# First SwiGLU of a hybrid encoder block: seven block products in place of eight, and the down product in passes over tokens

## The chip, the core and the metric

One core of a Trainium2 chip runs the whole block in one launch. The metric is the device time of one execution in microseconds. TensorE does the matrix products (PE in the profile, its weight loads PEld), VectorE (DVE), ScalarE (ACT) and GpSimd (POOL) the elementwise work, and SyncE (SP) issues most transfers between DRAM and the on-chip memory.

## The reference

One layer on 1024 tokens of width 1024: a SwiGLU half-step, a mixer (differential attention beside a bidirectional state-space part), a second SwiGLU half-step, a norm. The change is in the first SwiGLU:

```python
def swiglu(x, w_gate, w_up, w_down):
    return (jax.nn.silu(x @ w_gate) * (x @ w_up)) @ w_down
...
f = swiglu(rmsnorm(h, p["ffn1_pre_g"]), p["ffn1_w_gate"], p["ffn1_w_up"], p["ffn1_w_down"])
h = h + 0.5 * rmsnorm(f, p["ffn1_post_g"])
m = hybrid_mixer(rmsnorm(h, p["mix_pre_g"]), layer_idx, p)
```

The inner width is 2816, so gate and up are 1024 x 2816 and down is 2816 x 1024, all in float32.

## The kernel before

Every float32 product is made of three matmuls: an operand is split into a rounded part (hi, a CAST on ACT, line 127) and the rest (lo, a subtraction on DVE, line 128), and `mm3` (lines 130 to 135) adds hi·hi, hi·lo and lo·hi in PSUM. One matmul takes 128 rows of the sum and gives 128 x 512 outputs; there are 8 such rows of the width 1024 and 22 column tiles of 128 in the width 2816.

The first SwiGLU (`ffn`) goes over 11 chunks of two column tiles. In a chunk the gate and up weights, 128 x 1024 each, are loaded (`unit`, line 118), split, and multiplied with the transposed normed tokens, which lie on the chip as two halves of 512 tokens (`hT`). Products `pg` and `pu` (lines 230 to 235) have 24 matmuls each. The gate goes through silu on ACT (line 237), is multiplied by up on DVE (line 238) and split into `g`; then `down` (lines 242 to 256) multiplies `g` by two row tiles of the down weight, 12 matmuls for each tile of 128 tokens, and DVE adds the result to an accumulator on the chip (line 256). The first and the last chunk go in quarters of 256 tokens, so that the norms ahead (`norm_T`: Square on ACT, two small POOL steps, a scaling on DVE at line 161, eight transposes on PE at line 168) and the residual behind (`residual`, lines 187 to 193) lie among products. The column block z of the next projection (`proj_z`, 352 columns per matmul) fills in at the end, and `proj_conv` (product `pp`) follows.

A scheduler sets the order of the instructions on each engine. Each engine runs its own in that order and waits in place.

Of the kernel before, what the change touches and what calls it, by code (L numbers as in the profile page):

```python
# [91 lines left out]

class Kernel:
# [62 lines left out]
    def norm_T(self, pool, ps, h, xn, t, gain, halves, tag="pt"):  # L156
# [7 lines left out]
        for q in range(2):  # L164
            pt = ps.tile([P, 4, P], F32, tag=tag, name=tag, bufs=2)
# [897 lines left out]
def build(tc, a, out, stages="all"):  # L1063
    nc = tc.nc
    with ExitStack() as top:
# [15 lines left out]
        def norm_pools(ctx):  # L1081
            return k.pool(ctx, "nrm"), k.pool(ctx, "gains")
# [7 lines left out]
        ring = Ring(rp, 2, rp, 5, more=zp)  # L1090
        with ExitStack() as c1:
            nrm, gains = norm_pools(c1)
            ps = k.pool(c1, "ps1", space=PSUM)
# [195 lines left out]
```

## Time and profile before

| | |
|---|---|
| median of 3 runs | 2681.29 us (2681.08 to 2683.89) |
| the profiled execution | 2680.65 us, its span 2678.9 us |
| PE busy | 2584.6 us, 96% of the span |
| DVE, ACT, POOL busy | 1398.6, 905.1, 660.5 us |
| first SwiGLU and z, first product to first `pp` | 14.14 to 800.68 us |

The first and the last us of the span are its first and last instruction. A matmul's row has its start and a duration that runs on under the next one, so the pace of PE is read from the distance of two starts. Line numbers are those of the kernel above.

### The profile page before, as it was taken

How to read it: one execution, taken by the hardware profiler on the slowest of the kernel's cores; microseconds unless marked ns; L12 is line 12 of the kernel's file. 1: busy time of each engine (PE TensorE's matmuls, PEld its weight loads, DVE VectorE, ACT ScalarE, POOL GpSimd, SP SyncE). 2: the span in 40 equal slices, each digit the busy share in tenths (PEclk: the TensorE clock that was granted, in tenths of full speed). 3: DMA queues.
4: the chain of work that ended last, by engine and by line, in shares of the span. 5: the costliest groups of instructions: out<-in, count | busy, mean ns of one | idle time of the engine just before them, and what ended most of it. 6: DMA issues, size and time to landing. Idle time of an engine off the chain costs nothing.

```text
span 2678.9 us, 33127 instructions
## 1 busy us (share of the span) xinstructions
PE 2584.6 (96%) x13104; PEld 2186.3 (82%) x13104; DVE 1398.6 (52%) x1995; ACT 905.1 (34%) x1523; POOL 660.5 (25%) x644
## 2 busy tenths in 40 slices
PE   8999999999999999999988999999999999999996
PEld 7888888888988889777767888888888888888885
DVE  4233333333474743677637888888732333333336
ACT  4311111111144543444426555555431111111113
POOL 2000000000140184343426666666400000000005
PEclk9999999999999999999999999999999999999998
DMA  5211111111142465655454444442321111111112
GB/s 181 63 47 48 48 48 51 51 48 47 41 153 96 129 214 206 207 188 182 150 162 118 124 112 115 118 123 79 138 94 38 48 48 47 48 47 48 50 46 102
DMA packets 110652, 261.37 MB, mean 98 GB/s; under 512 B 11169, under 2 KB 51745, under 8 KB 105633
## 3 DMA queue, kind: packets, MB, share of 16 engines
q1 hardware_dynamic: 92160, 197.65, 22.6%
q0 software_dynamic: 10016, 57.42, 7.9%
q10 hardware_dynamic: 8320, 4.19, 0.5%
q8 instruction: 103, 1.69, 0.3%
q14 instruction: 53, 0.43, 0.1%
HBM read 191.32 MB, written 67.90 MB: 97 GB/s over the span
## 4 chain that ended last, share of the span: by engine, by line
PE 82%; DVE 6%; ACT 3%; POOL 3%; DMA 3%; issue 3%; SPq 0%; DVEq 0%; POOLq 0%; ACTq 0%
PE po L133 6%; PE po L135 6%; PE po L134 6%; PE pg L133 6%; PE pg L134 6%; PE pg L135 6%; PE pu L134 6%; PE pu L135 6%; PE pu L133 6%; PE pp L133 5%; PE pp L135 5%; PE pp L134 5%; PE pgu L133 2%; PE pgu L135 2%; PE pgu L134 2%
## 5 line engine op out<-in xcount | busy, mean ns | idle before, releaser
L256 DVE TENSOR_TENSOR acc<-acc,po 128x512 f32<-128x512 f32 x320 | 217.3, 686 | 433.4 <-PE po L135 433.0
L152 POOL TENSOR_SCALAR rstd<-rstd 128x1 f32<-128x1 f32 x64 | 30.4, 475 | 1451.4 <-ACT junk L151 1450.8
L128 DVE TENSOR_TENSOR split<-raw,split 128x1024 fp32r<-128x1024 f32 (+1 forms) x133 | 161.5, 1220 | 172.8 <-ACT split L127 172.8
L133 PE MATMUL pu<-hT,split 128*128 128x512 f32 (+1 forms) x624 | 223.6, 358 | 1.5 <-DVE sg L238 1.5
L133 PE MATMUL pg<-hT,split 128*128 128x512 f32 (+1 forms) x624 | 224.6, 360 | 0.3 <-ACT hT L127 0.2
L134 PE MATMUL pg<-hT,split 128*128 128x512 f32 (+1 forms) x624 | 224.4, 360 | 0.0
L135 PE MATMUL pg<-hT,split 128*128 128x512 f32 (+1 forms) x624 | 223.9, 359 | 0.0
L134 PE MATMUL pu<-hT,split 128*128 128x512 f32 (+1 forms) x624 | 223.4, 358 | 0.0
L135 PE MATMUL pu<-hT,split 128*128 128x512 f32 (+1 forms) x624 | 223.1, 358 | 0.0
L127 ACT CAST g<-sg 128x512 fp32r<-128x512 f32 (+1 forms) x104 | 57.5, 553 | 481.6 <-DVE sg L238 189.5
L127 ACT CAST split<-raw 128x1024 fp32r<-128x1024 f32 (+1 forms) x136 | 138.7, 1025 | 237.7 <-PE pu L135 83.6
L800 ACT ACTIVATE e<-sc,st 128x1024 f32<-128x1024 f32 x128 | 143.5, 1121 | 164.5 <-DVE st L796 159.9
L133 PE MATMUL pp<-hT,split 128*128 128x512 f32 x384 | 153.6, 400 | 9.5 <-DVE o L665 9.5
L238 DVE TENSOR_TENSOR sg<-sg,pu 128x512 f32<-128x512 f32 (+1 forms) x104 | 62.9, 605 | 185.4 <-PE pu L135 184.7
L796 DVE TENSOR_REDUCE st<-sc 128x1 f32<-128x1024 f32 x128 | 150.7, 1218 | 12.6 <-PE sc L794 12.5
L135 PE MATMUL pp<-hT,split 128*128 128x512 f32 x384 | 152.2, 396 | 0.0
L134 PE MATMUL pp<-hT,split 128*128 128x512 f32 x384 | 151.8, 395 | 0.0
L237 ACT ACTIVATE sg<-pg 128x512 f32<-128x512 f32 (+1 forms) x104 | 55.3, 532 | 271.2 <-PE pg L135 271.1
L133 PE MATMUL po<-odd,g 128*128 128x512 f32 x352 | 138.8, 396 | 6.8 <-DVE acc L256 6.8
L134 PE MATMUL po<-split,g 128*128 128x512 f32 x352 | 139.0, 395 | 0.0
L133 PE MATMUL po<-split,g 128*128 128x512 f32 x352 | 138.9, 396 | 0.1
L135 PE MATMUL po<-odd,g 128*128 128x512 f32 x352 | 138.4, 395 | 0.0
(314 smaller groups left out, 6653.8 us busy)
## 6 DMA issues: line engine op xcount, KB each, us to landing
raw<-in_w_gate_dram SPq DMA_DIRECT2D x44, 512.0 KB
raw<-in_w_up_dram SPq DMA_DIRECT2D x44, 512.0 KB
raw<-in_w_down_dram SPq DMA_DIRECT2D x44, 512.0 KB
qkd<-o SPq DMA_DIRECT2D x64, 256.0 KB
qk<-qkd POOLq DMA_DIRECT2D x16, 1024.0 KB, 7.8
x<-in_x_dram SPq DMA_DIRECT2D x16, 512.0 KB
h<-acc SPq DMA_DIRECT2D x16, 512.0 KB
vd<-o SPq DMA_DIRECT2D x32, 256.0 KB
```

The source lines that it names most:

```text
L127: self.nc.scalar.copy(out=hi, in_=src)
L128: (eng or self.nc.vector).tensor_tensor(out=lo, in0=src, in1=hi.bitcast(F32), op=ALU.subtract)
L133: mm(out=out, lhsT=a[0], rhs=b[0], start=start, stop=False)
L134: mm(out=out, lhsT=a[0], rhs=b[1], start=False, stop=False)
L135: mm(out=out, lhsT=a[1], rhs=b[0], start=False, stop=stop)
L152: nc.gpsimd.tensor_scalar(out=r[:, 1:2], in0=r[:, 0:1], scalar1=k / n, scalar2=k * EPS, op0=ALU.mult, op1=ALU.add)
L237: nc.scalar.activation(out=sg, in_=pg, func=AF.Silu)
L238: nc.vector.tensor_tensor(out=sg, in0=sg, in1=pu, op=ALU.mult)
L256: nc.vector.tensor_tensor(out=a[:, ns], in0=a[:, ns], in1=po[n], op=ALU.add)
L796: nc.vector.tensor_reduce(out=X["st"][:, j:j + 1], in_=pc, op=ALU.max, axis=AX.X, negate=True)
L800: self.nc.scalar.activation(out=X["e", j], in_=X["sc", j], func=AF.Exp, bias=st[:, j:j + 1], accum_out=st[:, 2 + j:3 + j])
```

## The change

Gate and up are each treated as a 2 x 2 block product (Strassen, in Winograd's form): the width 1024 in two halves of four rows, the 22 column tiles in two sets (i and i + 11), the tokens in two halves. Seven block products of 12 matmuls give the two column tiles for all tokens, for which the kernel before takes four products of 24. The sums of weight blocks (`s1` to `s4`) are made on POOL for each of the 22 pairs (`matrix`). The sums of token blocks (`t1` to `t4`) are made once in `blocks_prep`, on POOL and DVE, and transposed and split like the tokens. The rows of tokens 0 to 3 give two blocks each, those of tokens 4 to 7 five. Two products of the first pairs need tokens 0 to 3 alone (`begun`, `held`) and stand ahead of the rest. The results are combined from PSUM on DVE and ACT, and silu(gate)·up goes to DRAM (`gd`). `blocks_down` then reads it back three times, for tokens 0 to 2, 3 to 5 and 6 to 7; in each pass it loads and splits the whole down weight and sums all 22 row tiles in PSUM, two banks for each token tile. The accumulators on the chip are gone. The rest of the program, with the second SwiGLU, has the same functions.

```diff
+    def blocks_prep(self, tags, kept, junk, ps, src, gain, C, t):
+        nc = self.nc
+        V, G = nc.vector, nc.gpsimd
+        x = kept[t] if t < 4 else tags.tile([P, D], F32, "x", "x", 2)
+        nc.sync.dma_start(out=x, in_=src[t * P:(t + 1) * P, :])
+        r = self.rstd(tags, x, junk=junk())
+        V.scalar_tensor_tensor(out=x, in0=x, scalar=r, in1=gain, op0=ALU.mult, op1=ALU.mult)
+        ts = slice(t % 4 * P, (t % 4 + 1) * P)
+        def turn(n, s):
+            pt = ps.tile([P, 4, P], F32, "b", "pt", 8)
+            for i in range(4):
+                nc.tensor.transpose(out=pt[:, i, :], in_=s[:, i * P:(i + 1) * P], identity=self.ident)
+            self.split(pt, C[n][:, 0, :, ts], C[n][:, 1, :, ts])
+        x0, x1 = x[:, 0:512], x[:, 512:1024]
+        if t < 4:
+            turn("b11", x0)
+            turn("b21", x1)
+            return
+        y = kept[t - 4]
+        t1, t2, t3, t4 = (tags.tile([P, 512], F32, f"t{i}", f"t{i}", 1) for i in range(4))
+        G.tensor_tensor(out=t1, in0=x0, in1=y[:, 0:512], op=ALU.subtract)
+        V.tensor_tensor(out=t2, in0=x1, in1=t1, op=ALU.subtract)
+        G.tensor_tensor(out=t3, in0=x1, in1=x0, op=ALU.subtract)
+        G.tensor_tensor(out=t4, in0=y[:, 512:1024], in1=t2, op=ALU.subtract)
+        for n, v in (("b22", x1), ("t1", t1), ("t2", t2), ("t3", t3), ("t4", t4)):
+            turn(n, v)
...
+        def product(p, u, n, more=False):
+            for d in range(4):
+                ds = slice(d * P, (d + 1) * P)
+                self.mm3(p, (u[0][:, ds], u[1][:, ds]), (C[n][:, 0, d, :], C[n][:, 1, d, :]), d == 0 and not more, d == 3, skip_group_check=more)
+        def store(sg, f, h):
+            nc.sync.dma_start(out=gd[f][:, h * 512:(h + 1) * 512], in_=sg)
...
+        def begun(i):
+            for w in (wg, wu):
+                r = raw(w[i])
+                p = bank()
+                u = spool.tile([P, 512], F32, tag="u", name="u", bufs=2)
+                product(p, unit(r[:, 0:512], G), "b11")
+                A.copy(out=u, in_=p)
+                product(p, unit(r[:, 512:1024], G), "b21", True)
+                first.append((u, None, None))
+                if w is wg:
+                    sg = gate11(p, spool.tile([P, 512], F32, tag="s", name="s", bufs=3))
+                else:
+                    up11(p, sg, i)
+        def held(i, banks):
+            for w, b in zip((wg, wu), banks):
+                r = ring.load(1024)[:, 0:512]
+                nc.sync.dma_start(out=r, in_=w[i][:, 0:512])
+                p = ps.at(b, [P, 512], "b")
+                product(p, unit(r, G), "b11")
+                first.append((None, p, b))
+        def matrix(w, i, final):
+            u, p1, kept = first.pop(0) if first else (None, None, None)
+            whole = u is None
+            r0, r1 = raw(w[i]), raw(w[i + 11])
+            a11, a12, a21, a22 = r0[:, 0:512], r0[:, 512:1024], r1[:, 0:512], r1[:, 512:1024]
+            s1, s2, s4 = (spool.tile([P, 512], F32, tag="s", name="s", bufs=3) for _ in range(3))
+            s3 = a21
+            G.tensor_tensor(out=s1, in0=a21, in1=a22, op=ALU.add)
+            G.tensor_tensor(out=s2, in0=s1, in1=a11, op=ALU.subtract)
+            G.tensor_tensor(out=s3, in0=a11, in1=a21, op=ALU.subtract)
+            G.tensor_tensor(out=s4, in0=a12, in1=s2, op=ALU.subtract)
+            if whole:
+                u = tile()
+                if p1 is None:
+                    p1 = bank()
+                    product(p1, unit(a11), "b11")
+                A.copy(out=u, in_=p1)
+            p6, p5, p7 = bank(), bank(), bank()
+            product(p6, unit(s2), "t2")
+            V.tensor_tensor(out=u, in0=u, in1=p6, op=ALU.add)
+            product(p5, unit(s1), "t1")
+            c22 = tile()
+            V.tensor_tensor(out=c22, in0=u, in1=p5, op=ALU.add)
+            product(p7, unit(s3), "t3")
+            V.tensor_tensor(out=c22, in0=c22, in1=p7, op=ALU.add)
+            final(i + 11, 1, c22)
+            if whole:
+                product(p1, unit(a12), "b21", True)
+                final(i, 0, p1)
+                if kept is not None:
+                    ps.turn.append(kept)
+            product(p5, unit(s4), "b22", True)
+            c12 = tile()
+            V.tensor_tensor(out=c12, in0=u, in1=p5, op=ALU.add)
+            final(i, 1, c12)
+            product(p7, unit(a22), "t4", True)
+            V.tensor_tensor(out=u, in0=u, in1=p7, op=ALU.add)
+            final(i + 11, 0, u)
...
+    def blocks_down(self, ring, gp, fp, ps, gd, wd, post, fill):
+        nc = self.nc
+        order = [f for i in range(NF // 2) for f in (i, i + NF // 2)]
+        ps.turn = [6, 7]
+        for t0, n in ((0, 3), (3, 3), (6, 2)):
+            banks = [[ps.at(2 * t + h, [P, 512], "po") for h in range(2)] for t in range(n)]
+            for k, f in enumerate(order):
+                if k in (1, 3, 5, 7, 9, 11):
+                    self.move()
+                src = gd[f][:, t0 * P:(t0 + n) * P]
+                if t0 == 0 and k < 3:
+                    g = self.unit(ring, src, 3 * P)
+                else:
+                    raw = gp.tile([P, 3 * P], F32, tag="graw", name="graw", bufs=3)[:, :n * P]
+                    nc.sync.dma_start(out=raw, in_=src)
+                    g = gp.tile([P, 2, 3 * P], F32R, tag="gs", name="gs", bufs=4)[:, :, :n * P]
+                    self.split(raw, g[:, 0, :], g[:, 1, :])
+                dn = self.unit(ring, wd[f], 1024)
+                for t in range(n):
+                    ts = slice(t * P, (t + 1) * P)
+                    for h in range(2):
+                        ns = slice(h * 512, (h + 1) * 512)
+                        self.mm3(banks[t][h], (g[:, 0, ts], g[:, 1, ts]), (dn[:, 0, ns], dn[:, 1, ns]), k == 0, k == NF - 1)
+            for t in range(n):
+                f = fp.tile([P, D], F32, tag="f", name="f", bufs=4)
+                nc.scalar.copy(out=f[:, 0:512], in_=banks[t][0])
+                nc.vector.tensor_copy(out=f[:, 512:1024], in_=banks[t][1])
+                post(t0 + t, f)
+        ps.turn = [4, 5, 6, 7]
+        while self.running:
+            next(fill, None)
+            self.move()
+        for _ in fill:
+            pass
...
+            ps = Banks(k.pool(c1, "ps1", space=PSUM))
+            with ExitStack() as cb:
+                xp = k.pool(cb, "blocks")
+                h0, h1b = k.new_halves()
+                C = dict(b11=h0[:, :, 0:4, :], b21=h0[:, :, 4:8, :], b22=h1b[:, :, 0:4, :], t1=h1b[:, :, 4:8, :])
+                C.update({n: xp.tile([P, 2, 4, 512], F32R, name=n) for n in ("t2", "t3", "t4")})
+                spool = k.pool(cb, "sums")
+                tags = Tags(k.pool(cb, "work"), 5)
+                def early(begun, held):
+                    g = tags.tile([P, D], F32, "gain", "gain", 1)
+                    nc.sync.dma_start(out=g, in_=a["ffn1_pre_g"].partition_broadcast(P))
+                    kept = [r.bitcast(F32)[:, i, :] for r in (ring.take(1024) for _ in range(2)) for i in range(2)]
+                    def junk():
+                        return spool.tile([P, D], BF16, tag="s", name="junk", bufs=3)
+                    ps.turn = [0, 1, 2, 3]
+                    for t in range(T):
+                        k.blocks_prep(tags, kept, junk, ps, a["x"], g, C, t)
+                        if t == 3:
+                            begun(0)
+                        elif t in (4, 5):
+                            held(t - 3, (2 * t - 4, 2 * t - 3))
+                k.blocks_gate_up(ring, tags, spool, ps, C, a["w_gate1"], a["w_up1"], k.gd, early)
...
-            def pre1(t0):
-                for t in range(t0, t0 + 2):
-                    x = k.load_rows(nrm, a["x"], t)
-                    if t == 0:
-                        g1["pre"] = k.gain(gains, a["ffn1_pre_g"])
-                    k.push(k.norm_T(nrm, ps, x, x, t, g1["pre"], halves, "po" if t == 1 else "pt"))
-                k.finish()
-                if t0 == T - 2:
+            z = k.proj_z(zp, ring, ps, halves, dtr, (2,), "b", 8)
+            def post1(t, f):
+                if t == 0:
                     g1["post"] = k.gain(gains, a["ffn1_post_g"])
                     g1["mix"] = k.gain(gains, a["mix_pre_g"])
-            z = k.proj_z(zp, ring, ps, halves, dtr, (2,), "pgu", 4)
-            def post1(t, acc):
-                k.push(k.residual(nrm, acc, t, a["x"], g1["post"], 0.5, h1, nc.gpsimd,
-                                  lambda f, x, t: k.norm_T(nrm, ps, f, x, t, g1["mix"], halves)))
-                if t >= 4:
-                    next(z)
-            gp = k.pool(c1, "gp")
-            k.ffn(ring, ring, lambda: gp.tile([P, 2, 1024], F32R, tag="g", name="g", bufs=2),
-                  lambda: gp.tile([P, 512], F32, tag="sg", name="sg", bufs=2), ps, k.new_acc(k.pool(c1, "acc")), halves, a["w_gate1"], a["w_up1"], a["w_down1"], pre1, post1)
-            k.finish()
-            for _ in z:
-                pass
+                k.push(k.residual(nrm, f, t, a["x"], g1["post"], 0.5, h1, nc.gpsimd,
+                                  lambda f, x, t: k.norm_T(nrm, ps, f, x, t, g1["mix"], halves, "b", 8)))
+            k.blocks_down(ring, gp, fp, ps, k.gd, a["w_down1"], post1, z)
+            k.nx = 3
```

ACT in the first stage of the program, before (x is a row tile of tokens; junk,rstd is its Square):

```order
7 L151 ACTIVATE junk,rstd<-x 128x1024 x2
8 L127 CAST split<-raw 128x1024
9 L151 ACTIVATE junk,rstd<-x 128x1024
10 L237 ACT_TABLE_LOAD
11 L237 ACTIVATE sg<-pg 128x256
12 L127 CAST split<-raw 128x1024 x2
13 L127 CAST hT_100<-pt 128x4x128 x2
14 L127 CAST g<-sg 128x256
15 L237 ACTIVATE sg<-pg 128x256
16 L151 ACTIVATE junk,rstd<-x 128x1024
```

ACT there now (w_269, w_353 and w_437 are the rows of tokens 4, 5 and 6; b a product, L330 the silu of the first gate product):

```order
8 L172 CAST split<-raw 128x512
9 L172 CAST hT_98<-pt 128x4x128 x3
10 L172 CAST split<-raw 128x512 x3
11 L344 COPY u<-b 128x512 x2
12 L330 ACT_TABLE_LOAD
13 L330 ACTIVATE s<-b 128x512
14 L196 ACTIVATE junk,rstd<-w_269 128x1024
15 L196 ACTIVATE junk,rstd<-w_353 128x1024
16 L172 CAST hT_99<-pt 128x4x128 x2
17 L172 CAST t_100<-pt 128x4x128
18 L172 CAST t_101<-pt 128x4x128
```

The Squares of tokens 4 to 7 now stand behind the copies and the silu of the first products, where before they stood between splits.

POOL in the same stage, before (rstd belongs to a row tile, L191 to the residual at the stage's end):

```order
24 L152 TENSOR_SCALAR rstd<-rstd 128x1
25 L153 TENSOR_TENSOR rstd<-rstd,mhalf 128x1
26 L152 TENSOR_SCALAR rstd<-rstd 128x1
27 L153 TENSOR_TENSOR rstd<-rstd,mhalf 128x1
28 L152 TENSOR_SCALAR rstd<-rstd 128x1
29 L153 TENSOR_TENSOR rstd<-rstd,mhalf 128x1
30 L191 TENSOR_TENSOR acc_108<-x,acc_108 128x1024
31 L152 TENSOR_SCALAR rstd<-rstd 128x1
```

POOL there now (L280 to L283 are token sums, w_486 the row of token 7; L368 to L371 weight sums of the first pair; L197 and L198 in this stretch are token 7's norm):

```order
32 L280 TENSOR_TENSOR w_445<-w_437,split 128x512
33 L282 TENSOR_TENSOR w_446<-w_437 128x512
34 L368 TENSOR_TENSOR s<-raw 128x512
35 L197 TENSOR_SCALAR rstd<-rstd 128x1
36 L283 TENSOR_TENSOR w_446<-split,w_445 128x512
37 L369 TENSOR_TENSOR s<-s,raw 128x512
38 L370 TENSOR_TENSOR raw<-raw 128x512
39 L198 TENSOR_TENSOR rstd<-rstd,mhalf 128x1
40 L371 TENSOR_TENSOR s<-raw,s 128x512
41 L280 TENSOR_TENSOR w_494<-w_486,split 128x512
42 L282 TENSOR_TENSOR w_495<-w_486 128x512
```

The weight sums of the first pair now stand between the two steps of token 7's norm and ahead of its token sums.

SP in the down products, before (one load of 512 KB a row):

```order
60 L118 DMA raw<-in_w_up_dram 128x1024 x2
61 L118 DMA raw<-in_w_down_dram 128x1024
62 L118 DMA raw<-in_w_gate_dram 128x1024
63 L118 DMA raw<-in_w_down_dram 128x1024
64 L118 DMA raw<-in_w_gate_dram 128x1024
65 L118 DMA raw<-in_w_up_dram 128x1024 x2
66 L118 DMA raw<-in_w_down_dram 128x1024
67 L118 DMA raw<-in_w_gate_dram 128x1024
68 L118 DMA raw<-in_w_down_dram 128x1024
```

SP in the third pass now (graw is a piece of gd of 128 KB, h_69 a finished row of the residual, L238 its store):

```order
183 L163 DMA raw<-in_w_down_dram 128x1024
184 L436 DMA graw<-gd 128x256
185 L238 DMA h_69<-f 128x1024
186 L163 DMA raw<-in_w_down_dram 128x1024
187 L436 DMA graw<-gd 128x256
188 L238 DMA h_69<-f 128x1024
189 L163 DMA raw<-in_w_down_dram 128x1024
190 L436 DMA graw<-gd 128x256
191 L163 DMA raw<-in_w_down_dram 128x1024
192 L436 DMA graw<-gd 128x256
193 L226 DMA x<-in_x_dram 128x1024
194 L163 DMA raw<-in_w_down_dram 128x1024
```

Each down weight of 512 KB now comes with a piece of the stored product, and row stores stand between them.

## Rows read from the trace of the kernel before

**Rows 1.** The page: busy time by engine, and the chain that ended last by engine.

```profile
PE 2584.6 (96%) x13104; PEld 2186.3 (82%) x13104; DVE 1398.6 (52%) x1995; ACT 905.1 (34%) x1523; POOL 660.5 (25%) x644
...
PE 82%; DVE 6%; ACT 3%; POOL 3%; DMA 3%; issue 3%; SPq 0%; DVEq 0%; POOLq 0%; ACTq 0%
```

**Rows 2.** Timeline of PE, a steady chunk: start us, duration us, engine, line, op.

```profile
200.23 0.39 PE L133 MATMUL pu<-hT,split 128*128 128x512 f32 x1
...
202.50 0.39 PE L134 MATMUL pu<-hT,split 128*128 128x512 f32 x1
...
203.20 0.40 PE L134 MATMUL po<-split,g 128*128 128x512 f32 x1
...
205.52 0.40 PE L135 MATMUL po<-split,g 128*128 128x512 f32 x1
```

**Rows 3.** The same view in the second SwiGLU, weights in another tile.

```profile
2046.67 0.40 PE L135 MATMUL pu<-hT,v 128*128 128x512 f32 x1
...
2047.37 0.39 PE L135 MATMUL pu<-hT,v 128*128 128x512 f32 x1
```

**Rows 4.** Timeline of PE, the first products of the program.

```profile
14.14 0.58 PE L133 MATMUL pg<-hT,split 128*128 128x256 f32 x1 [0.24 <-ACT hT L127]
...
16.10 0.41 PE L133 MATMUL pg<-hT,split 128*128 128x256 f32 x1
...
17.17 0.41 PE L135 MATMUL pg<-hT,split 128*128 128x256 f32 x1
...
18.39 0.28 PE L134 MATMUL pu<-hT,split 128*128 128x256 f32 x1
...
19.23 0.28 PE L134 MATMUL pg<-hT,split 128*128 128x256 f32 x1
```

**Rows 5.** Stretches: length, busy us (x instructions) per engine, PEclk, DMA share, GB/s.

```profile
14.00:18.00 4.00, 3.86 (x19) 3.85 (x20) 1.47 (x4) 3.32 (x7) 3.83 (x4) 1.00 1.02 405
200.00:300.00 100.00, 100.00 (x437) 81.78 (x436) 33.55 (x44) 14.84 (x20) 0.00 (x0) 1.00 0.13 43
736.00:801.00 65.00, 60.47 (x384) 56.20 (x383) 51.13 (x55) 31.52 (x57) 31.71 (x43) 1.00 0.42 148
938.00:1005.00 67.00, 67.00 (x327) 57.16 (x326) 33.47 (x33) 27.47 (x37) 56.69 (x55) 1.00 0.69 215
```

**Rows 6.** Timeline of PE, where the stage ends (pp is the next stage).

```profile
799.25 0.32 PE L133 MATMUL pgu<-split,hT 128*128 128x352 f32 x1
...
800.68 0.39 PE L133 MATMUL pp<-hT,split 128*128 128x512 f32 x1
```

**Rows 7.** The chain that ended last, in order of time: start us, us, what.

```profile
2.18 6.22 DMA x<-in_x_dram
...
41.37 0.87 PE pt L168 x8
```

**Rows 8.** Groups by line, 0 to 760 us: busy us, mean ns, idle before.

```profile
L256 DVE TENSOR_TENSOR acc<-acc,po 128x512 f32<-128x512 f32 x156 | 106.1, 686 | 227.9 <-PE po L135 227.5
L128 DVE TENSOR_TENSOR split<-raw,split 128x1024 fp32r<-128x1024 f32 (+1 forms) x67 | 80.8, 1208 | 102.6 <-ACT split L127 102.6
...
L128 DVE TENSOR_TENSOR hT<-pt,hT 128x512 fp32r<-128x512 f32 x20 | 13.6, 687 | 11.2 <-ACT hT L127 11.2
...
L191 POOL TENSOR_TENSOR acc<-x,acc 128x1024 f32<-128x1024 f32 x5 | 12.0, 2405 | 1.4 <-DVE acc L190 1.4
L127 ACT CAST hT<-pt 128x512 fp32r<-128x512 f32 x20 | 11.1, 583 | 7.0 <-PE pt L168 7.0
```

**Rows 9.** Timeline, the first row tile of x on ACT and DVE.

```profile
5.33 1.06 ACT L151 ACTIVATE junk<-x 128x1024 bf16<-128x1024 f32 x1 [3.25 <-DMA x<-in_x_dram]
...
7.43 1.28 DVE L161 SCALAR_TENSOR_TENSOR x<-x,rstd,gain 128x1024 f32<-128x1024 f32 x1 [7.43 <-POOL rstd L153]
```

**Rows 10.** Timeline, one POOL sum and the DVE instruction beside it.

```profile
736.56 2.41 POOL L191 TENSOR_TENSOR acc<-x,acc 128x1024 f32<-128x1024 f32 x1
...
736.63 3.42 DVE L161 SCALAR_TENSOR_TENSOR x<-acc,rstd,gain 128x1024 f32<-128x1024 f32 x1
```

More of the change, by code (lines that the diff above doesn't have):

```diff
@@ L90, in tile, with __init__, whole, at @@
         return r[-1]
+class Tags:
+    def __init__(self, pool, n):
+        self.pool, self.n = pool, n
+        self.place = dict(x=(0, 2), gain=(2, 1), t0=(3, 1, 0), t1=(3, 1, 1), t2=(4, 1, 0), t3=(4, 1, 1))
+        self.turn, self.made, self.half, self.next = {}, {}, None, 0
+    def whole(self, i):
+        return self.pool.tile([P, D], F32, tag=f"w{i}", name=f"w{i}", bufs=1)
+    def tile(self, shape, dtype, tag, name, bufs):
+        if tag == "rstd":
+            return self.pool.tile(shape, dtype, tag=tag, name=name, bufs=bufs)
+        if tag == "c":
+            if self.half is None:
+                self.half = self.whole(self.next % self.n)
+                self.next += 1
+                return self.half[:, 0:512]
+            h, self.half = self.half, None
+            return h[:, 512:1024]
+        first, n, *part = self.place[tag]
+        if not part:
+            k = self.turn[tag] = (self.turn.get(tag, -1) + 1) % n
+            return self.whole(first + k)
+        if part[0] == 0:
+            self.made[first] = self.whole(first)
+        return self.made[first][:, part[0] * 512:(part[0] + 1) * 512]
+class Banks:
+    def __init__(self, ps):
+        self.ps, self.turn = ps, list(range(8))
+    def tile(self, shape, dtype, tag, name, bufs):
+        i = self.turn.pop(0)
+        self.turn.append(i)
+        return self.at(i, shape, name)
+    def at(self, i, shape, name):
+        return self.ps.tile(shape, F32, tag=f"b{i}", name=name, bufs=1)
 class Kernel:
@@ L154, in rstd, with norm_T @@
         return r[:, 0:1]
-    def norm_T(self, pool, ps, h, xn, t, gain, halves, tag="pt"):
+    def norm_T(self, pool, ps, h, xn, t, gain, halves, tag="pt", bufs=2):
         nc = self.nc
@@ L164, in norm_T @@
         for q in range(2):
-            pt = ps.tile([P, 4, P], F32, tag=tag, name=tag, bufs=2)
+            pt = ps.tile([P, 4, P], F32, tag=tag, name=tag, bufs=bufs)
             for i in range(4):
@@ new lines, in half_units, with take, unit, blocks_gate_up @@
+    def half_units(self, ring):
+        def take():
+            while True:
+                sp = ring.take(1024)
+                for h in range(2):
+                    yield sp[:, 0, h * 512:(h + 1) * 512], sp[:, 1, h * 512:(h + 1) * 512]
+        units = take()
+        def unit(src, eng=None):
+            u = next(units)
+            self.split(src, *u, eng)
+            return u
+        return unit
+    def blocks_gate_up(self, ring, cp, spool, ps, C, wg, wu, gd, early):
+        nc = self.nc
+        V, G, A = nc.vector, nc.gpsimd, nc.scalar
+        unit = self.half_units(ring)
+        def raw(src):
+            t = ring.load(1024)
+            nc.sync.dma_start(out=t, in_=src)
+            return t
+        def tile():
+            return cp.tile([P, 512], F32, tag="c", name="c", bufs=10)
+        def bank():
+            return ps.tile([P, 512], F32, "b", "b", 8)
+        def product(p, u, n, more=False):
[4 more added lines that the diff above has]
+            nc.sync.dma_start(out=gd[f][:, h * 512:(h + 1) * 512], in_=sg)
+        def gate11(p, sg):
+            A.activation(out=sg, in_=p, func=AF.Silu)
+            return sg
+        def up11(p, sg, i):
+            V.tensor_tensor(out=sg, in0=sg, in1=p, op=ALU.mult)
+            store(sg, i, 0)
+        def begun(i):
[56 more added lines that the diff above has]
+            final(i + 11, 0, u)
+        first = []
+        early(begun, held)
+        for i in range(NF // 2):
+            kept = {}
+            def silu(f, h, c):
+                if (f, h) == (i, 0):
+                    kept[f, h] = gate11(c, tile())
+                else:
+                    A.activation(out=c, in_=c, func=AF.Silu)
+                    kept[f, h] = c
+            def mult(f, h, c):
+                sg = kept[f, h]
+                V.tensor_tensor(out=sg, in0=sg, in1=c, op=ALU.mult)
+                store(sg, f, h)
+            matrix(wg, i, silu)
+            matrix(wu, i, mult)
@@ L1090, in build @@
         ring = Ring(rp, 2, rp, 5, more=zp)
+        k.gd = dr([NF, P, S], F32, name="gd")
         with ExitStack() as c1:
+            ps = Banks(k.pool(c1, "ps1", space=PSUM))
[20 more added lines that the diff above has]
+                k.blocks_gate_up(ring, tags, spool, ps, C, a["w_gate1"], a["w_up1"], k.gd, early)
```

14 lines of the change are left out of this document (9 added, 5 removed).

## The prediction

> **What bounds the kernel now.** I read the page first: PE is busy 96% of the span and has 82% of the chain that ended last [rows 1]. So time is won where PE has fewer columns to stream, and lost where it waits. Next the table by stretches: between 200 and 300 us PE is busy 100 of 100 us at the full granted clock, while DVE has 33.55, ACT 14.84 and POOL nothing, and DMA moves 43 GB/s [rows 5]. The middle of the first SwiGLU is bound by PE alone, and the other engines have room. Then the timeline, because a matmul's duration overlaps the next: ten starts of products from 200.23 to 202.50 give 0.227 us for a matmul of 512 columns, ten of the down product from 203.20 to 205.52 give 0.232 [rows 2]; 256 columns take (19.23 - 18.39) / 7 = 0.120 [rows 4], the 352 columns of z (800.68 - 799.25) / 9 = 0.159 [rows 6], a transpose 0.87 / 8 = 0.109 [rows 7].
>
> The stage runs from the first product at 14.14 [rows 4] to the first `pp` at 800.68 [rows 6]: 786.5 us. Its matmuls, counted from the loops: nine chunks of 192 products, 1728 x 0.227 = 392.3; the first and the last chunk with 768 of half width, x 0.120 = 92.2; down 11 x 96 = 1056 x 0.232 = 245.0; z 192 x 0.159 = 30.5; of 128 transposes all but the first 16, x 0.109 = 12.2. Sum 772.2. The other 14.3 us are the slow pace at first (0.214 for half a matmul, from 16.10 to 17.17 [rows 4]) and waits, of which 4.5 lie in the last 65 us [rows 5].
>
> **Products.** 22 pairs x 7 x 12 = 1848 matmuls of full width take the place of 2112, with the half-width ones counted as halves. At an unchanged pace this removes 264 x 0.227 = 59.9, and the half widths another 92.2 - 384 x 0.227 = 5.0. The pace can change, since the tiles do: with the weights in another tile, three starts from 2046.67 to 2047.37 give 0.233 [rows 3]. The ends are 0.227 and 0.234; I take 0.229, near the tile pair that stays in four of seven products, so 3.7 us come back (ends 0 and 12.9). Down keeps 1056 matmuls, with the same two operands: 245.0.
>
> **Feeding the products.** A weight pair now gives PE 84 x 0.229 = 19.2 us of work. In that time DVE has seven half-width splits at 0.69 or less, five additions like line 256 at 0.686 and two products: 9.6 us; ACT some ten passes at 0.583, 5.8; POOL four sums of half of 2.405 [rows 8], 4.8; DMA two loads and two to three stores, under 90 GB/s. All this lies under PE. Splits can run some ten half units ahead, and a weight's second load waits only for a split 1.5 pairs earlier, so I put the steady feeding at nothing. At the first two or three pairs the lead is not there yet: 3 us (0 to 10). Inside a pair a bank is written again 24 products (5.4 us) after its first sum, and DVE has to read it between: two additions, 1.4 us. That is hidden; if DVE came later than 5.4 us, PE would stop there.
>
> A row speaks against so much POOL work: a DVE scaling that takes 1.28 us alone [rows 9] took 3.42 when a POOL sum of 2.41 had begun 0.07 us ahead [rows 10], so it stood nearly to the sum's end. The Trainium skill (SBUF — State Buffer, Who interferes with whom) makes this a rule: a DVE instruction with two inputs in SBUF contends with a GpSimd instruction that reads SBUF. That holds for splits of weights too, which no row here shows beside a POOL sum. By that rule DVE would stand up to 4.8 us more in each pair, 14.4 of 19.2; the sum would not change by it, but the slow rival below gets its footing.
>
> **The start.** Here the change costs. The second row of x landed at 8.40 [rows 7], the first at 5.33 [rows 9], with the gain between: 1.54 us for each 512 KB. Now the gain comes first and four rows are needed: 5.33 + 4 x 1.54 = 11.5. Square to scaling takes 7.43 - 5.33 = 2.1 [rows 9]. ACT then has, from about 12.7, eight token casts and five of weights at 0.58, so the first product can begin at some 19.7 us, 5.5 later than before. The 96 early products, at half pace for some 3.4 us as before [rows 4], keep PE until about 43, with token 4's transposes until 45.
>
> In ACT's order the Squares of tokens 4 and 5 stand behind the silu of the first gate product, that is behind the 50th matmul: 19.7 + 3.4 + 42.5 x 0.227 = 32.7, though the later of the two rows is there at 11.5 + 4.5 x 1.54 = 18.4, behind two weights and a half. Token 6 reuses token 4's tile, freed by transposes behind 87 early matmuls, at 41.5; a load of 4 us (between 1.5, the bare transfer, and 6.2 in a queue [rows 7]), 2.1 and the scaling of 1.28 bring 48.9. POOL then has, in its order and ahead of token 7's scaling, three token sums of token 6 and three weight sums, 6 x 1.2 = 7.2; with the norm's last small step and the scaling of 1.28 it is 58. Token 7's three POOL sums, one DVE difference held up beside them, a transpose and a cast: 5.4. I let the main products begin at 64 us. Ends: 52, if loads are quick and the POOL sums fall beside other work, and 72. All but some 9 us of transposes between 45 and 64 PE is idle, so its clock falls and the slow first products are paid again: 1.7.
>
> **The seam, the passes, the tail.** The first loads of the stored product wait for memory that the last products hold, and for stores behind them in SP's order; three pieces go through the old ring, 12.5 us of cover. The first down banks wait for one or two DVE reads: 2 us (0 to 4). A step of the first two passes is 18 matmuls, 4.18 us, of the third 12, 2.78. It needs one weight split of 1.21 on DVE [rows 8] and one of a third as much, as much on ACT, and 720 or 655 KB by DMA, 172 and 236 GB/s. The trace has 215 GB/s over 67 us with PE full and 405 in a short stretch [rows 5]. I cost the passes at nothing, with the lead of six split buffers; the end is 10. At the end z fills 30.5 us beside the last two token tiles' norms: 5 lost (2 to 10), near the 4.5 of before.
>
> **The sum.** 64 + (1848 - 96) x 0.229 = 401.2 + slow pace 1.7 + first pairs 3 + down 245.0 + seam 2 + z 30.5 + 64 transposes 7.0 + tail 5 = 759.4, against 800.7: 41.3 us. Behind the stage the order of PE is the same but for a few neighbours, so nothing is added. The profiled execution took 2680.65; less 41.3 is 2639.4, and the median lies 0.6 above that execution: 2640.
>
> **Rivals.** *The start costs nothing.* Main products at 52 with a pace of 0.227 and no waits at the first pairs, the seam and the tail: 12 + 3.5 + 3 + 2 + 3 = 23.5 less, 2617. For it: the rows of x are on the chip long before their Squares. Against it: the POOL order has twelve 1.2 us sums in a chain with tile reuse.
>
> *The passes starve.* Three raw buffers, each held for landing (6.2 us for a queued row [rows 7]), ACT, and DVE 1.21 [rows 8], give a weight every (6.2 + 2.4) / 3 = 2.9 us at best, and SP waits in place at row stores. With 9 us to land it is 3.8 in place of 2.78: 22 us in the third pass, less part of the lead; 15 to 25 us, some 2660. For it: 236 GB/s is above all that the trace holds for long. Against it: DMA's share was 0.69 at 215.
>
> *Slower than before: DVE sets the pace of the pairs.* If each POOL sum holds a DVE instruction, as in rows 10, and ACT, DVE and PE wait for each other in order, a pair takes longer than PE's 19.2 us. It decides from 41 / 22 = 1.9 us a pair on; at 3 us a pair, 66 us, the time is 2640 + 66 = 2706. For it: DVE at 14.4 of 19.2 and reads between PE's writes to one bank. Against it: 5.4 us of slack at each such read, and a DVE load that is three quarters at worst.
>
> **Chances.** Forecast 0.52, cheap start 0.20, starving passes 0.18, slower 0.07, and 0.03 that losses add up to no change. The range takes the first three: 2617 to 2668. What a measurement of this kernel can tell from no change is about 0.2%, 5 us: faster 0.90, the same 0.03, slower 0.07.
>
> **What would show it.** Between 100 and 450 us the profile after should have PE full with a pace of 0.227 to 0.234 between starts; the first main product (on `t2`) near 64 us, with PE nearly empty from 45; POOL busy a quarter of those stretches; down steps of 4.2, 4.2 and 2.8 us without waits for `raw` or `graw`; the first `pp` near 759. I am wrong if PE waits for DVE additions in every pair, if the third pass shows waits for splits, or if `pp` comes early because the main products began before 55.

## The result, and the profile after

The changed kernel takes 2637.29 us, median of four runs (2636.05 to 2638.77), against 2681.64 (2681.08 to 2683.89) for the kernel before in the same rounds: ratio 0.9833, 95% interval 0.9816 to 0.985. The forecast was 2640. The profiled executions, 2680.65 and 2636.05, differ by 44.6 us. The first `pp` starts at 756.52, against 800.68 [rows 6]: 44.16 us earlier. So all but 0.4 us of the gain lies in the first SwiGLU and z.

The page of the kernel after, busy time and the chain by engine, answers to [rows 1]:

```profile
PE 2523.7 (96%) x12504; PEld 2122.4 (81%) x12504; DVE 1521.7 (58%) x2123; ACT 1003.9 (38%) x1709; POOL 825.1 (31%) x750
...
PE 82%; DVE 6%; POOL 3%; ACT 3%; issue 2%; DMA 2%; SPq 0%; DVEq 0%; POOLq 0%; ACTq 0%
```

PE lost 60.9 us of busy time and kept its share and its place in the chain. DVE, ACT and POOL together gained 387 us, and their shares of the chain are what they were. The table by stretches of the kernel after says why, beside [rows 5] (length, busy us and instructions of PE, PEld, DVE, ACT and POOL, granted clock, DMA share, GB/s):

```profile
45.00:71.00 26.00, 13.17 (x66) 10.09 (x65) 22.24 (x25) 13.78 (x25) 20.08 (x18) 0.63 0.19 67
...
200.00:300.00 100.00, 100.00 (x443) 82.81 (x442) 56.96 (x73) 30.17 (x53) 29.72 (x20) 1.00 0.23 79
...
469.00:575.00 106.00, 106.00 (x461) 86.15 (x460) 57.05 (x60) 47.94 (x68) 11.78 (x12) 1.00 0.64 213
575.00:670.00 95.00, 95.00 (x423) 77.37 (x422) 55.42 (x62) 42.28 (x66) 16.43 (x15) 1.00 0.61 200
670.00:719.00 49.00, 49.00 (x224) 40.05 (x223) 34.86 (x45) 27.04 (x42) 5.51 (x4) 1.00 0.82 273
719.00:757.00 38.00, 34.26 (x213) 32.87 (x213) 16.24 (x21) 14.28 (x25) 13.45 (x24) 1.00 0.26 91
...
52.00:71.00 19.00, 9.74 (x40) 7.43 (x41) 16.96 (x19) 9.53 (x17) 16.38 (x13) 0.50 0.17 56
```

In the products (200 to 300) and in the three passes (469 to 719) PE is full. It is not full in one long stretch, 45 to 71 us: 13.17 of 26, at a granted clock of 0.63 on the mean; from 52 to 71 us, where PE is busy for 9.74 of 19 us with transposes between waits, it is 0.50, the lower level of 1.2 GHz. The timeline of PE after shows the first and the last early product, the end of that stretch, the steady pace, the change to the down products and the end of the stage (start us, us):

```profile
20.93 1.08 PE L178 MATMUL b<-hT,split 128*128 128x512 f32 x3
...
44.87 0.39 PE L180 MATMUL b<-hT,split 128*128 128x512 f32 x1
...
71.04 0.78 PE L178 MATMUL b<-t,split 128*128 128x512 f32 x1
71.61 0.63 PE L179 MATMUL b<-t,split 128*128 128x512 f32 x1
72.04 0.56 PE L180 MATMUL b<-t,split 128*128 128x512 f32 x1
72.44 0.40 PE L178 MATMUL b<-t,split 128*128 128x512 f32 x1
...
200.09 0.39 PE L180 MATMUL b<-t,split 128*128 128x512 f32 x1
...
202.36 0.39 PE L178 MATMUL b<-hT,split 128*128 128x512 f32 x1
...
468.92 0.39 PE L178 MATMUL po<-split 128*128 128x512 f32 x1
...
481.17 0.40 PE L178 MATMUL po<-split,gs 128*128 128x512 f32 x1
...
482.10 0.39 PE L179 MATMUL po<-split,gs 128*128 128x512 f32 x1
...
719.06 0.40 PE L180 MATMUL po<-split,gs 128*128 128x512 f32 x1
...
756.36 0.32 PE L180 MATMUL b<-split,hT 128*128 128x352 f32 x1
756.52 0.39 PE L178 MATMUL pp<-hT,split 128*128 128x512 f32 x1
```

The main products begin at 71.04. Three starts are slow, then the pace is (202.36 - 200.09) / 10 = 0.227 on the new tile `t`, as it was on `hT` before. The other 1749 products up to the first down product at 468.92 take (468.92 - 72.44) / 1749 = 0.2267 each, with no gap over 0.3 us on the way. The last down product starts at 719.06, the first of z one pitch later, at 719.29.

### The profile page after: what moved, and what is told of

Read it like the earlier page. It is cut to its first block, busy times and chain, and to the rows that moved or that the text cites. A ratio compares the mean times of both kernels' runs of the same rounds, so it can differ in the third digit from the quotient of the medians.

```text
span 2634.3 us, 32969 instructions
## 1 busy us (share of the span) xinstructions
PE 2523.7 (96%) x12504; PEld 2122.4 (81%) x12504; DVE 1521.7 (58%) x2123; ACT 1003.9 (38%) x1709; POOL 825.1 (31%) x750
## 4 chain that ended last, share of the span: by engine, by line
PE 82%; DVE 6%; POOL 3%; ACT 3%; issue 2%; DMA 2%; SPq 0%; DVEq 0%; POOLq 0%; ACTq 0%
PE po L180 7%; PE po L178 7%; PE po L179 7%; PE b L178 5%; PE b L179 5%; PE b L180 5%; PE pp L178 5%; PE pp L180 5%; PE pp L179 5%; PE pg L178 3%; PE pg L179 3%; PE pg L180 3%; PE pu L179 3%; PE pu L178 3%; PE pu L180 3%
## 5 line engine op out<-in xcount | busy, mean ns | idle before, releaser
L197 POOL TENSOR_SCALAR rstd<-rstd 128x1 f32<-128x1 f32 x64 | 32.2, 503 | 986.8 <-ACT junk L196 985.8
L173 DVE TENSOR_TENSOR split<-raw,split 128x1024 fp32r<-128x1024 f32 (+3 forms) x218 | 250.3, 1154 | 128.4 <-ACT split L172 127.6
L172 ACT CAST split<-raw 128x1024 fp32r<-128x1024 f32 (+3 forms) x227 | 192.8, 860 | 231.0 <-issue 77.4
L502 DVE TENSOR_TENSOR acc<-acc,po 128x512 f32<-128x512 f32 x160 | 108.6, 686 | 209.6 <-PE po L180 209.5
L178 PE MATMUL po<-odd,g 128*128 128x512 f32 x352 | 139.0, 397 | 6.8 <-DVE acc L502 6.8
L180 PE MATMUL po<-odd,g 128*128 128x512 f32 x352 | 138.4, 395 | 0.0
L179 PE MATMUL po<-odd,g 128*128 128x512 f32 x352 | 138.2, 393 | 0.0
L178 PE MATMUL b<-hT,split 128*128 128x512 f32 x352 | 137.0, 390 | 0.0
L179 PE MATMUL b<-hT,split 128*128 128x512 f32 x352 | 136.9, 389 | 0.0
L180 PE MATMUL b<-hT,split 128*128 128x512 f32 x352 | 136.9, 389 | 0.0
L1053 POOL TENSOR_SCALAR e<-e,st 128x768 f32<-128x768 f32 x64 | 75.6, 1181 | 181.5 <-DVE st L1052 136.7
L179 PE MATMUL po<-split,gs 128*128 128x512 f32 x334 | 131.9, 395 | 0.0
L180 PE MATMUL po<-split,gs 128*128 128x512 f32 x334 | 131.9, 395 | 0.0
L178 PE MATMUL po<-split,gs 128*128 128x512 f32 x334 | 131.3, 395 | 0.0
L172 ACT CAST g<-sg 128x512 fp32r<-128x512 f32 (+1 forms) x52 | 28.8, 553 | 243.7 <-DVE acc L502 124.8
L1055 POOL TENSOR_TENSOR e<-e,e 128x768 f32<-128x768 f32 x64 | 118.3, 1848 | 5.4
L178 PE MATMUL pp<-split,hT 128*128 128x512 f32 (+1 forms) x320 | 117.5, 368 | 0.0
```

What stands on the lines that cost most here:

```text
L172: self.nc.scalar.copy(out=hi, in_=src)
L173: (eng or self.nc.vector).tensor_tensor(out=lo, in0=src, in1=hi.bitcast(F32), op=ALU.subtract)
L178: mm(out=out, lhsT=a[0], rhs=b[0], start=start, stop=False, **kw)
L179: mm(out=out, lhsT=a[0], rhs=b[1], start=False, stop=False, **kw)
L180: mm(out=out, lhsT=a[1], rhs=b[0], start=False, stop=stop, **kw)
L197: nc.gpsimd.tensor_scalar(out=r[:, 1:2], in0=r[:, 0:1], scalar1=k / n, scalar2=k * EPS, op0=ALU.mult, op1=ALU.add)
```

## The experiments

Times are medians; ratios are against the kernel before in the same rounds. Behind the first `pp` nothing was edited, yet that part of the profiled span goes from 1873.8 to 1881.6 us (1877.8 in the changed kernel). So edits of the first SwiGLU are compared by the first `pp` rather than by the time. Kernels with the same code up to the main products begin these at 71.04 to 72.26, so a microsecond there can't be told apart.

**Eight products, three passes.** Gate and up in the eight classical block products, without sums; down as in the changed kernel.

```diff
-            product(p6, unit(s2), "t2")
-            V.tensor_tensor(out=u, in0=u, in1=p6, op=ALU.add)
...
+            product(p, u11, "b12")
+            product(p, u12, "b22", True)
+            final(i, 1, p)
+            u21, u22 = unit(r1[:, 0:512]), unit(r1[:, 512:1024])
+            for h, (m, n) in enumerate((("b11", "b21"), ("b12", "b22"))):
+                p = bank()
+                product(p, u21, m)
+                product(p, u22, n, True)
+                final(i + 11, h, p)
```

> Gate and up by eight block products again (2112 matmuls of 512 columns), no token or weight sums, five of the seven transposed token blocks gone down to four; store to DRAM and the three passes of down as in the changed kernel. Theory (the time comes from matmuls alone, the passes cost nothing, the start is what Strassen pays): products begin near 21 us and run without the idle stretch of 45 to 71 us; 20.9 + 2112 x 0.2267 = 478.8 + slow pace 1.7 + 32 transposes 3.5 + down with its transposes 250.4 + tail 37.2 gives the first pp at 792.5 against 756.5, so 36 us slower than the changed kernel, about 2673, and 8 us faster than before. Rival (the gain is that of the passes: no accumulators on DVE, one PSUM sum over 22 row tiles): as fast as the changed kernel or faster by its idle start, 2615 to 2637.

Measured: 2677.58 us, ratio 0.9987 (0.9978 to 0.9997). PE after this edit, in the hole of its start, where its unbroken products begin, and where the stage ends:

```profile
52.10 1.94 PE L270 MATMUL pt<-ident,w 128*128 128x128 f32 x8 [4.53 <-DVE w L264]
...
56.24 0.78 PE L178 MATMUL b<-hT,split 128*128 128x512 f32 x1
...
511.79 0.39 PE L178 MATMUL po<-split 128*128 128x512 f32 x1
...
799.54 0.39 PE L178 MATMUL pp<-hT,split 128*128 128x512 f32 x1
```

The theory wanted the first `pp` at 792.5. It allowed for no hole in the start; but after 108 products PE waits 4.53 us for DVE's scaling of token 6, and the rest begin at 56.24, six of them slow. So the layout and the passes alone are worth 1.1 us at the first `pp`; the other 43.0 come with the seven products. These would be 264 x 0.2267 = 59.9, but the main products start at 71.04 and not at 56.24, with 12 fewer done ahead: 59.9 - 14.8 - 2.7 = 42.4. So more than a quarter of the saving, 17.5 us, goes into the start.

**The norms of tokens 4 and 5 ahead of the first products.**

```diff
...
+                    next(prep[4])
+                    next(prep[5])
+                    begun(0)
...
```

> The loads, Squares and scalings of tokens 4 and 5 are written ahead of the first products, so that ACT does the Squares among the token casts near 13 to 17 us and not behind the silu at 34.6. Theory (the queue on ACT and the tile reuse behind it set the start): token 6 can be loaded when its tile is freed among the early products, some 10 us sooner; the main products begin near 58 us in place of 71.0, time near 2624. Rival (the sums of tokens 4 to 7 and of the first pair fill POOL and DVE, which hold each other up, so the start is their throughput): main products at 66 to 71, 2632 to 2637.

Measured: 2640.28, ratio 0.9849 (0.9834 to 0.9864). The main products start at 68.30, 2.7 us earlier. Then PE waits 1.50 us for DVE, and the next fourteen products are 0.43 us apart, where three were slow in the changed kernel (PE, then the stretch in the columns used above, granted clock 0.50):

```profile
68.30 0.47 PE L178 MATMUL b<-t,split 128*128 128x512 f32 x1
70.27 0.79 PE L179 MATMUL b<-t,split 128*128 128x512 f32 x1 [1.50 <-DVE t L173]
```

```profile
70.30:75.00 4.70, 4.70 (x11) 3.73 (x12) 3.92 (x3) 1.86 (x3) 3.37 (x3) 0.50 0.10 17
```

The first `pp` is at 758.14. My theory, that the place of the Squares on ACT was the hold and its removal worth 13 us, fell. The 2.7 us that the order did win were lost in the wait and at the lower clock.

**Own rows for tokens 6 and 7**, so that their loads need not wait, at the price of 24 early products.

```diff
-        x = kept[t] if t < 4 else tags.tile([P, D], F32, "x", "x", 2)
+        x = kept[t] if t < 4 or t > 5 else tags.tile([P, D], F32, "x", "x", 2)
...
```

> The rows of tokens 6 and 7 get a tile of their own (a third split buffer), so they are loaded at the start and do not wait for the tiles of tokens 4 and 5; in exchange one pair of early products (24 matmuls, 5.4 us) goes behind the start. The Squares of tokens 4 to 7 still stand behind the silu at 34. Theory (tile reuse is what delays token 7): main products near 60 us, less 5.4 us of early work: net 5 us faster than the changed kernel, 2632. Rival (POOL and DVE throughput sets the start): main products near 70 and 5.4 us more to do, 2642.

Measured: 2645.39, ratio 0.987 (0.9853 to 0.9886); twelve products on `b11`, which now stand behind the start, begin at 74.16, those on `t2` at 79.51, `pp` at 766.97. The reuse of the tile was not the hold either.

**Both edits**, for all four tokens 4 to 7.

> The two earlier edits of the start together: the norms of tokens 4 to 7 all stand ahead of the first products, and tokens 6 and 7 have rows of their own (72 early products instead of 96). Theory 1 (each edit failed alone because the other hold was left: the early norms of 6 and 7 could not start for want of a row, and the own rows came behind the first products' work on ACT): the main products start near 57 us instead of 71.0, 24 early products (3.5 us) go out later, net 8 to 10 us less: 2626 to 2630. Rival (POOL and DVE have a fixed amount of work before the t-tiles are whole, and stretch each other, so the order changes nothing): main start 66 to 74, 2636 to 2645.

Measured: 2639.24, ratio 0.9844 (0.983 to 0.9857); twelve products on `b11` begin at 64.89, those on `t2` at 70.08, `pp` is at 757.94. The stretch before the products, in the columns used above:

```profile
45.00:71.00 26.00, 18.18 (x86) 14.02 (x86) 25.00 (x28) 14.45 (x27) 24.01 (x17) 0.74 0.22 71
```

With both holds gone DVE is busy 25.00 of 26 us and POOL 24.01, and the end is the same to 1.4 us. That is what the rival forecast: the work of POOL and DVE fills the stretch also with the norms ahead. It isn't shown that no order helps: part of DVE's work there is splits of the first weights, and no run moved these behind token 7's sums.

**All weight sums on DVE** (`s1` to `s4`).

```diff
-            G.tensor_tensor(out=s1, in0=a21, in1=a22, op=ALU.add)
...
+            V.tensor_tensor(out=s1, in0=a21, in1=a22, op=ALU.add)
...
```

> The four weight sums of each of the 22 pairs on DVE in place of POOL. Theory (PE sets the pace of the pairs, DVE has room; at the start POOL is freed of the sums of the first pairs that stand inside token 7's norm): pace of products unchanged at 0.227 us between 100 and 450 us with DVE near 60 to 65% busy, the main products begin 3 to 5 us earlier, 2633. Rival (DVE is near its limit in the pairs): PE waits in every pair, over 2645.

Measured: 2634.83, ratio 0.9832 (0.9818 to 0.9847), no measurable difference from the changed kernel. The half of the theory on the start failed: the main products begin at 70.17, 0.9 us earlier and not 3 to 5, and `pp` is at 757.13. Its middle:

```profile
200.00:300.00 100.00, 100.00 (x443) 82.80 (x442) 59.94 (x93) 29.55 (x52) 0.00 (x0) 1.00 0.23 79
```

DVE took 20 instructions more (93 against 73), 13.6 us at 0.68, yet its busy time rose by 3.0 only. So beside POOL's sums DVE had lost 10.6 us in 100, or 2.0 in a pair of 84 x 0.2267 = 19.04 us. PE is full either way.

**Both edits of the start, with the weight sums on DVE.**

> As the run before it, and all weight sums on DVE instead of POOL. Theory 1 (POOL's weight sums of the first pair stretch DVE at the start, and POOL's norm steps queue behind them): 1 to 3 us less than the run with the weight sums on POOL, and if that run has its start near 57, 2624 to 2628 here. Rival (DVE itself is the fuller engine at the start): 1 to 4 us more than that run. Either way the pace of the products between 100 and 450 us stays 0.227 us.

Measured: 2636.61, ratio 0.9835 (0.9821 to 0.9848), `pp` at 756.00: 1.9 us before the same kernel with the sums on POOL, as its theory said, and 0.5 before the changed kernel, which can't be told apart.

**No sums on POOL at all**: the token sums `t1`, `t3`, `t4` on DVE as well.

```diff
-        G.tensor_tensor(out=t1, in0=x0, in1=y[:, 0:512], op=ALU.subtract)
+        V.tensor_tensor(out=t1, in0=x0, in1=y[:, 0:512], op=ALU.subtract)
...
```

> The changed kernel with weight sums and the token sums t1, t3, t4 on DVE: POOL keeps the small norm steps and the splits of the early weights alone. Theory (POOL and DVE stretch each other when both read SBUF): DVE's scaling of token 7 takes 1.28 us instead of 2.28, its splits of 128x512 from SBUF 0.69 instead of 1.19 to 1.75; DVE gets 8.2 us of sums more (12 at 0.69) and about as much back, so the main products start at 66 to 71 and the time is 2630 to 2637. Rival (no stretching; those long instructions are long for another reason): the long durations stay, DVE is 8 us fuller of which 4 stand between token 6 and token 7, main start 74 to 76, 2638 to 2642.

Measured: 2640.84, ratio 0.9852 (0.9839 to 0.9866). First DVE, then POOL, in the timeline of the changed kernel before its main products:

```profile
49.60 2.14 DVE L264 SCALAR_TENSOR_TENSOR w<-w,rstd,w 128x1024 f32<-128x1024 f32 x1
...
59.55 0.69 DVE L173 TENSOR_TENSOR t<-pt,t 128x512 fp32r<-128x512 f32 x1
...
61.62 2.28 DVE L264 SCALAR_TENSOR_TENSOR w<-w,rstd,w 128x1024 f32<-128x1024 f32 x1 [0.45 <-POOL rstd L198]
63.83 2.35 DVE L173 TENSOR_TENSOR split<-raw,split 128x512 fp32r<-128x512 f32 x2
66.10 1.75 DVE L173 TENSOR_TENSOR split<-s,split 128x512 fp32r<-128x512 f32 x1
67.77 0.68 DVE L281 TENSOR_TENSOR w<-w,w 128x512 f32<-128x512 f32 x1
```

```profile
51.91 1.28 POOL L280 TENSOR_TENSOR w<-w,split 128x512 f32<-128x512 f32 x1 [1.25 <-DVE w L264]
...
58.91 1.71 POOL L370 TENSOR_TENSOR raw<-raw 128x512 f32<-128x512 f32 x1
60.59 1.00 POOL L198 TENSOR_TENSOR rstd<-rstd,mhalf 128x1 f32<-128x1 f32 x1
61.57 1.25 POOL L371 TENSOR_TENSOR s<-raw,s 128x512 f32<-128x512 f32 x1
64.05 1.58 POOL L280 TENSOR_TENSOR w<-w,split 128x512 f32<-128x512 f32 x1 [1.23 <-DVE w L264]
65.59 1.71 POOL L282 TENSOR_TENSOR w<-w 128x512 f32<-128x512 f32 x1
```

And DVE of the kernel without sums on POOL:

```profile
55.78 1.28 DVE L264 SCALAR_TENSOR_TENSOR w<-w,rstd,w 128x1024 f32<-128x1024 f32 x1 [0.72 <-POOL rstd L198]
...
61.19 0.68 DVE L173 TENSOR_TENSOR split<-s,split 128x512 fp32r<-128x512 f32 x1
...
65.39 1.28 DVE L173 TENSOR_TENSOR split<-raw,split 128x512 fp32r<-128x512 f32 x2
```

The scaling of token 7 takes 1.28 instead of 2.28, a split of a sum 0.68 instead of 1.75: the long durations come from POOL's sums beside them. But DVE now does all the work, without a break from 55.78 on, and the main products begin at 72.72. After the first of them come four more transposes and then eleven products at a slow pace, 0.43 us, and `pp` is at 761.51, 5.0 us later than in the changed kernel. The durations went as the theory said, start and time nearer to the rival: at the start, taking the token sums from POOL too gives DVE less back than it costs.

**Two raw buffers in the passes** instead of three.

```diff
+        raws, ring.raws = ring.raws, [x for x in ring.raws if x[1] == 2]
```

> The three passes of down with two raw weight buffers instead of three (restored after the passes). Theory (a raw buffer is held for the landing, 4 to 5 us, and for ACT 1.05 and DVE 1.22 with short waits: 6.5 to 7.5 us, so that two give a weight every 3.2 to 3.8 us): the first two passes, which want one every 4.2 us, do not change; the third wants one every 2.78 us and lacks 9 to 22 us over its 22 weights, less the 14 us for which six split buffers run ahead: 0 to 10 us more, 2637 to 2647, with waits of PE for splits of w_down after 690 us. Rival (the rate of the transfers and not the buffers decides, as with three): no change, 2636 to 2638, and no waits.

Measured: 2642.94, ratio 0.9859 (0.9846 to 0.9873), 5.7 us more than the changed kernel. ACT's weight splits in the third pass of this kernel:

```profile
697.41 1.05 ACT L172 CAST split<-raw 128x1024 fp32r<-128x1024 f32 x1 [2.12 <-DMA raw<-in_w_down_dram]
700.73 1.05 ACT L172 CAST split<-raw 128x1024 fp32r<-128x1024 f32 x1 [1.97 <-DMA raw<-in_w_down_dram]
...
715.31 1.05 ACT L172 CAST split<-raw 128x1024 fp32r<-128x1024 f32 x1 [1.87 <-DMA raw<-in_w_down_dram]
```

Seven splits from 697.41 to 715.31 are one every 2.98 us, less often than the step of 2.78 wants and a little better than the 3.2 expected. The last weight is split at 717.7, where the changed kernel has it at 704.1. PE, ACT and DVE of this kernel in z, and PE of the changed kernel at the same place:

```profile
739.06 0.66 PE L178 MATMUL b<-split,hT 128*128 128x352 f32 x1 [8.07 <-DVE dtr L601]
```

```profile
726.83 1.05 ACT L172 CAST split<-raw 128x1024 fp32r<-128x1024 f32 x1 [1.70 <-DMA raw<-in_w_xbc_dram]
727.79 1.06 ACT L448 COPY f<-po 128x512 f32<-128x512 f32 x2
```

```profile
734.64 4.18 DVE L235 SCALAR_TENSOR_TENSOR f<-f,rstd,gain 128x1024 f32<-128x1024 f32 x1 [0.72 <-POOL rstd L198]
738.74 0.27 DVE L601 COPY dtr<-b 128x32 f32<-128x32 f32 x2
```

```profile
729.02 0.43 PE L178 MATMUL b<-split,hT 128*128 128x352 f32 x1 [1.84 <-DVE dtr L599]
```

The passes take 2.1 us longer, from the first to the last down product, and z 6.8. In z the weights come late one after another: ACT splits one of the projection behind z before it copies the last down sums, so the norm of these rows is late, and with it DVE's 4.18 us scaling. Behind that stands DVE's copy of z's first results (`dtr`), for which PE waits 8.07 us instead of 1.84. The first `pp` is at 767.15, 10.6 later. Of this 1.7 was there before the passes began, and 3.8 came back behind the stage, so the time shows less. So the buffers set the rate here: each is held 2 x 2.98 = 5.96 us, by which (an estimate) three would give a weight every 2.0 us.

**One and two block products fewer**: what is the next limit?

```diff
-            product(p7, unit(a22), "t4", True)
+            unit(a22)
```

This leaves the product of `a22` with `t4` out of the result; the second kernel leaves out that of `s4` with `b22` too. Their splits and sums stay.

> The changed kernel without the second product of p7 (a22 on t4): that block product is left out of the result, its weight split stays. Theory (TensorE alone sets the pace of the first SwiGLU: nothing else is near its limit at 19.0 us for a matrix): 22 x 12 matmuls fewer at 0.2267 us, 59.9 us less than the changed kernel: 2577, with the pace in between unchanged. Rival (DVE, with 11 to 13 us of work in 19, or the three raw buffers, is near): waits of PE for splits or sums in every matrix, 2585 to 2610.

> As the run before it, and the second product of p5 (s4 on b22) left out too; splits and sums stay. Theory (TensorE still alone at 13.6 us for a matrix, DVE at 80 to 95%): 119.7 us less than the changed kernel, 2517 to 2520. Rival (DVE with 10.9 to 12.8 us of work for a matrix, and a raw buffer that comes free late, give no more than a matrix in 15 to 16 us): 2545 to 2570, with waits of PE for splits.

Measured: 2579.36 (ratio 0.962, 0.9606 to 0.9634) and 2518.59 (0.9397, 0.9381 to 0.9413): 57.9 and 118.7 us less than the changed kernel, for 59.9 and 119.7 expected. The middle with five products:

```profile
200.00:300.00 100.00, 100.00 (x442) 82.84 (x442) 72.30 (x102) 41.09 (x75) 43.62 (x31) 1.00 0.34 111
```

PE is still full, DVE at 72. Up to the down products PE waits once, 2.0 us at 157.1, for a copy on ACT. The theory holds.

## Why the prediction was right

The time and the mechanism were right: PE bounds the stage, the gain is the products that fall away less what the start costs, and feeding and passes stay hidden. What the terms measured, in us:

| term of the sum | predicted | measured after |
| --- | --- | --- |
| first product, early products end | 19.7, 43 | 20.93, 44.87 |
| main products start | 64 (52 to 72) | 71.04 |
| pace of a product | 0.229 | 0.227 |
| slow pace again | 1.7 | 0.8 |
| first pairs, seam | 3, 2 | 0, 0 |
| waits in the passes | 0 (end 10) | 0 |
| down, 1056 matmuls | 245.0 | 245.1 (719.29 - 468.92, less 48 transposes x 0.109) |
| tail beside z | 5 | 5 |
| first `pp` | 759.4 | 756.5 |

*The start* was mis-sized: 7 us too early, inside its ends. Token 6's scaling ended at 51.7, not 48.9. POOL then needed 9.7 us, to 61.6, for the six sums and the norm's last step, where six at 1.2 and that step were 7.8: two sums took 1.71 or more, and the step itself 1.00, stretched by DVE. Token 7's scaling took 2.28 for 1.28, and ahead of its difference DVE has three splits of weights in its order, 4.0 us stretched (the timelines above), which I had not counted. "PE nearly empty from 45" was wrong too: half the stretch, 13.17 of 26 us, is transposes, which from 52 on run at the lower clock. The slow pace behind it, 1.7 for 0.8, is no fixed price: it was three products here and fourteen with the early norms.

*The pace* stayed at the lower end, 0.227, on the new tile as well: 1752 x 0.0023 = 4 us won. The pace of [rows 3], which I let pull it up, belongs to another pair of tiles. *The first pairs* and *the seam* cost nothing: no gap is left at either place. These three, 9 us, and the start's 7 nearly cancel, so it is partly luck that the sum is off by only 3 us.

*The rivals.* Cheap start: an edit at each hold and two at both brought the first `pp` forward by 0.5 us at best, less than the starts of equal kernels differ by. Without the token and weight sums, in the eight products, the main products begin 14.8 us earlier: these sums, with their transposes and splits, are the price. Another order of the weights' part of it was not tried. Starving passes: with three buffers PE never waits, with two it does, so the mechanism is real. Its size was not: the rival held a buffer for 6.2 + 2.4 = 8.6 us, where the two buffers show 5.96. DVE as the bound: dead; with every weight sum on DVE, or with two products less to hide under, PE stays full but for the one wait of 2.0 us.

The Trainium skill (SBUF — State Buffer, Who interferes with whom) has a DVE instruction with two inputs in SBUF contend with a GpSimd instruction that reads SBUF, and calls this an exclusive lock. The traces agree: in the changed kernel, up to 400 us, 44 of the 132 DVE splits of 128x512 from SBUF take over 0.9 us, and every one of the 44 ends 0.55 us after the end of a POOL sum. The split of 66.10 above is one: it ends at 67.85, the POOL sum of 65.59 at 67.30. In the same stretch 51 of the 93 POOL sums take over 1.35 us, and each of these ends 1.12 to 1.16 us after the end of a DVE instruction with two inputs in SBUF. So each side stands until the other is done. The price in the steady part is smaller than the prediction's upper bound, 2.0 us in a pair, not 4.8, since 88 of the 132 splits met no POOL sum in this way.

No variant beats the changed kernel by more than the runs tell apart. What stays open is the 26 us at the start: nothing that was tried gives PE enough other work there.

## What to carry to other kernels

Fewer products pay in full only while the bound engine has none of the new work ahead of it: price the preparation that must be complete before the first product (here more than a quarter of the saving) apart from the steady feeding, which was free. Where a start is long, look at the busy time of the engines that feed it before reordering: here two engines came to 24 and 25 of 26 us, and no order of the norms helped. Where PE idles among short pieces of work, count the slow products behind the gap as well. Where weights are read several times, the number of load buffers can set the rate: take the time that one buffer is held, divide by the buffers, and compare with the step.

## What the runs showed of the hardware that was not expected

- Sums on POOL and DVE work with two inputs in SBUF stretch each other: on DVE 1.28 to 2.28 and 0.68 to 1.75, on POOL 1.25 to 1.71. Each waits for the end of the other's instruction. Splits from PSUM stay at 0.69 beside them, as that of `t<-pt` at 59.55 above.
- The pace of a matmul of 512 columns goes with the tile that an operand lies in: 54 down products with the stored product in the weight ring run at (481.17 - 468.92) / 54 = 0.227, those from 481.17 on, with it in its own tile `gs`, at (482.10 - 481.17) / 4 = 0.232. Shape and type are the same; why was not tried.
- DMA gave 273 GB/s for 49 us, at a share of 0.82, with PE full; the highest long stretch read before was 215 [rows 5].
